# An einsum kernel without its counting instructions, and with 10 KB read twice on eight DMA engines

## Chip, cores and metric

One core of one Trainium2 chip. The metric is device time in microseconds (us) of one execution, the median of several. The profile's *span* runs from the first to the last instruction of the program; the time of an execution is 1.7 to 2.2 us longer than its span, and this difference turns out to matter. Before: 262.18 us, median of 3 runs (261.52 to 262.26).

## The reference

```python
def setup_inputs():
    batch, m, k, n = 16, 512, 768, 1024
    return {"x": randn(batch, k, m), "y": randn(batch, k, n)}      # float32

def reference(x, y):
    return np.einsum('bkm,bkn->bmn', x, y).astype(np.float32)
```

Per batch the core reads 1.5 MB of x and 3 MB of y and writes 2 MB: 109 MB in all.

## The kernel before

VectorE casts x and y to bf16, TensorE multiplies, ScalarE copies PSUM to SBUF, and SyncE issues every transfer. Loads are double buffered; the store of batch b-4 is issued behind the load of batch b. What the change and the argument touch:

```python
    LAG = 4
    NO = 5                                     # output buffers
    ...
    idle = ec(nc.semaphore("idle"))
    ...
    for b in range(B):                         # SyncE
        i = b % 2
        if b >= 2:
            nc.sync.wait_ge(cast, nx[b - 2])
        wide_dma("x", xs[i][:], x_v[b], 4, True).then_inc(sx[i], 16)
        if b >= 2:
            nc.sync.wait_ge(cast, nx[b - 2] + parts(b - 2))
        wide_dma("y", ys[i][:], y_v[b], 2, True).then_inc(sy[i], 16)
        if b >= LAG:
            store(b - LAG)
    for b in range(B - LAG, B - 1):
        store(b)

    for _ in range(60):                        # VectorE counts; nobody waits for it
        nc.vector.sem_inc(idle, 1)
    for b in range(B):
        ...                                    # wait for x, cast; wait for y, cast

    nc.scalar.nop().then_inc(room, 2)
    for _ in range(60):                        # ScalarE counts
        nc.scalar.sem_inc(idle, 1)
    for b in range(B):
        ...                                    # wait for PE, copy PSUM to ob
```

Of the kernel before, what the change touches and what calls it, by code (L numbers as in the profile page):

```python
# [1 line left out]

_os.environ.setdefault("NEURON_RT_ULTRASERVER_MODE", "4")

# [2 lines left out]

# [5 lines left out]


@with_exitstack
def kernel(
    ctx: ExitStack,
    tc: tile.TileContext,
    x: bass.AP,
    y: bass.AP,  # L20
    out: bass.AP,
):
    nc = tc.nc
    P = 128
    FP32 = mybir.dt.float32
    BF16 = mybir.dt.bfloat16

    B, K, M = x.shape
    _, _, N = y.shape
    KT = K // P  # L30
    MT = M // P
    NF = 512
    NT = N // NF



    x_v = x.rearrange("b (p ko) m -> b p ko m", ko=KT)
    y_v = y.rearrange("b (p ko) n -> b p ko n", ko=KT)
    o_v = out.rearrange("b (p mo) n -> b p mo n", mo=MT)

    LAG = 4
    NO = 5
    KH = KT // 2

    section = ExitStack()
    section.enter_context(tc.tile_critical())
    ec = ctx.enter_context
    xs = [ec(nc.sbuf_tensor(f"xs{i}", [P, KT, M], FP32)) for i in range(2)]
    ys = [ec(nc.sbuf_tensor(f"ys{i}", [P, KT, N], FP32)) for i in range(2)]
    xb = ec(nc.sbuf_tensor("xb", [P, 2, KT, M], BF16))  # L50
    yb = ec(nc.sbuf_tensor("yb", [P, 2, KT, N], BF16))
    ob = [ec(nc.sbuf_tensor(f"ob{i}", [P, MT, N], FP32)) for i in range(NO)]

    HB = MT // 2
    ps = [ec(nc.psum_tensor(f"ps{i}", [P, HB, NT, NF], FP32)) for i in range(2)]
    sx = [ec(nc.semaphore(f"sx{i}")) for i in range(2)]
    sy = [ec(nc.semaphore(f"sy{i}")) for i in range(2)]
    so = [ec(nc.semaphore(f"so{i}")) for i in range(NO)]
    cast = ec(nc.semaphore("cast"))
    ready = ec(nc.semaphore("ready"))  # L60
    room = ec(nc.semaphore("room"))
    groups = ec(nc.semaphore("groups"))
    idle = ec(nc.semaphore("idle"))
    outs = ec(nc.semaphore("outs"))


    made = {}

    def wide_dma(key, dst, src, dram_rows, load):


        if key not in made:
            made[key] = nc.sync.dma_start(dst, src)
            return made[key]
        pat = mybir.BassSymbolicTensorAccessPattern
        widen = lambda a: a.rearrange("(q r) k m -> q (r k m)", r=dram_rows)
        plain = lambda a: a.rearrange("p k m -> p (k m)")
        s, d = (widen(src), plain(dst)) if load else (plain(src), widen(dst))
        return nc.sync.add_instruction(_copy.replace(
            made[key].ins, name=nc.get_next_instruction_name(),  # L80
            ins=(pat(ap=s.ap, dtype=s.dtype, bass_ap=s, is_dma=False),),
            outs=(pat(ap=d.ap, dtype=d.dtype, bass_ap=d, is_dma=False),),
            sync_info=None, ant_dge_precooked=False))


    def parts(b):
        return 2 if b in (15,) else 1


    nx = [sum(1 + parts(a) for a in range(b)) + 1 for b in range(B)]  # L90


    def store(b):


        if b < B - 2:
            nc.sync.wait_ge(groups, 2 * (b + 2))
        else:
            nc.sync.wait_ge(outs, b - (B - 3))
        nc.sync.dma_start(o_v[b], ob[b % NO][:]).then_inc(so[b % NO], 16)  # L100

    for b in range(B):
        i = b % 2
        if b >= 2:
            nc.sync.wait_ge(cast, nx[b - 2])
        wide_dma("x", xs[i][:], x_v[b], 4, True).then_inc(sx[i], 16)
        if b >= 2:
            nc.sync.wait_ge(cast, nx[b - 2] + parts(b - 2))
        wide_dma("y", ys[i][:], y_v[b], 2, True).then_inc(sy[i], 16)
# [3 lines that stand above are left out]
        store(b)  # L113


    for _ in range(60):
        nc.vector.sem_inc(idle, 1)
    for b in range(B):
        i = b % 2
        n = 16 * (b // 2 + 1)  # L120
        if b >= 2:
            nc.vector.wait_ge(groups, 2 * (b - 1))
        nc.vector.wait_ge(sx[i], n)
        nc.vector.tensor_copy(xb[:, i], xs[i][:]).then_inc(cast, 1)  # L124
        nc.vector.wait_ge(sy[i], n)
        for h in range(parts(b)):
            ks = slice(h * KT // parts(b), (h + 1) * KT // parts(b))
            nc.vector.tensor_copy(yb[:, i, ks], ys[i][:, ks]).then_inc(cast, 1)  # L128


    for b in range(B):
        nc.gpsimd.wait_ge(cast, nx[b]).then_inc(ready, 1)
        for h in range(parts(b)):
            nc.gpsimd.wait_ge(cast, nx[b] + h + 1).then_inc(ready, 2 // parts(b))


    x_w = xb[:].rearrange("p s k (j mo) -> p s k mo j", mo=MT)
    pe = OrderedEngineSet([nc.tensor.engine])
    with nc.Fori(0, B // 2, engines=pe):
        with nc.Fori(0, 2, engines=pe) as s:  # L140
            nc.tensor.wait_ge(ready, 2).then_inc(ready, -2)
            for mo in range(MT):
                g, m = divmod(mo, HB)
                if m == 0:
                    nc.tensor.wait_ge(room, 1).then_inc(room, -1)  # L145
                for kt in range(KT):
                    if mo == 0 and kt == KH:
                        nc.tensor.wait_ge(ready, 1).then_inc(ready, -1)
                    for nt in range(NT):
                        mm = nc.tensor.matmul(  # L150
                            ps[g][:, m, nt], x_w[:, bass.ds(s, 1), kt, mo],
                            yb[:, bass.ds(s, 1), kt, nt * NF:(nt + 1) * NF],
                            start=(kt == 0), stop=(kt == KT - 1))
                if m == HB - 1:
                    mm.then_inc(groups, 1)


    nc.scalar.nop().then_inc(room, 2)
    for _ in range(60):
        nc.scalar.sem_inc(idle, 1)  # L160
    for b in range(B):
        if b >= NO:
            nc.scalar.wait_ge(so[b % NO], 16 * (b // NO))
        for g in range(2):
            nc.scalar.wait_ge(groups, 2 * b + g + 1)
            cp = nc.scalar.copy(ob[b % NO][:, g * HB:(g + 1) * HB].rearrange("p m (t f) -> p m t f", f=NF),  # L166
                                ps[g][:])
            if b < B - 1:
                cp.then_inc(room, 1)
        if b == B - 2:  # L170
            nc.scalar.drain().then_inc(outs, 1)
    cp.then_inc(outs, 1)

    for b in range(B - LAG - 1, B - 2):
        nc.sync.wait_ge(so[b % NO], 16 * (b // NO + 1))
    section.close()




    nc.sync.dma_start(o_v[B - 1], ob[(B - 1) % NO][:])


# [1 line left out]
_INS = ['x', 'y']  # L185
_OUTS = [((16, 512, 1024), 'float32')]


# [23 lines left out]
```

## Time and profile before

| | before |
|---|---|
| time, median | 262.18 us |
| span of the profiled execution | 260.7 us (an execution of 262.47 us) |
| TensorE busy | 71% |
| DMA queue 1, share of 16 engines | 98.1% |
| instruction packets of queue 14 in the span | 2 |

### The profile page before, as it was taken

What the parts mean: (1) busy time and instruction counts of PE and PEld (TensorE: products, weight loads), DVE (VectorE), ACT (ScalarE), POOL (GpSimd) and SP (SyncE); (2) the same over time, 40 slices, a digit from 0 to 9 for tenths busy, and PEclk for the clock granted to TensorE, in tenths of its full rate; (3) what the DMA queues carried; (4) which work ended last, traced back from release to release, by engine and by line L of the source; (5) the groups of instructions that cost most, each with busy time, mean ns of one, the idle gap of its engine ahead of it and who ended that gap; (6) DMA issues with size and microseconds to landing.
All of it is one profiled execution on the core that took longest, in us unless ns stands there. A gap on an engine that the chain in (4) does not pass through costs nothing. (4 is left out here: it accounts for less than half of the span.)

```text
span 260.7 us, 2506 instructions
## 1 busy us (share of the span) xinstructions
PE 186.1 (71%) x768; PEld 89.8 (34%) x768; DVE 82.0 (31%) x33; ACT 61.1 (23%) x33; POOL 0.2 (0%) x4
## 2 busy tenths in 40 slices
PE   0009999998937949479596894969959197696910
PEld 0004555554512515124242351434425043253500
DVE  0261644525222252312524115252142522225000
ACT  1000442243220222202214022040322205022220
POOL 0000000000000000000000000000000000000000
PEclk9999999999995999959889797797999889799985
DMA  7998999999899899989999989999998999999994
GB/s 260 432 494 385 468 385 468 392 392 488 385 410 493 370 450 475 427 385 405 483 400 437 465 367 453 410 483 402 410 485 382 445 468 417 410 410 430 427 410 181
DMA packets 4514, 109.07 MB, mean 418 GB/s; under 512 B 768, under 2 KB 768, under 8 KB 768
## 3 DMA queue, kind: packets, MB, share of 16 engines
q1 hardware_dynamic: 4512, 109.05, 98.1%
q14 instruction: 2, 0.02, 0.0%
HBM read 75.50 MB, written 33.55 MB: 418 GB/s over the span
## 5 line engine op out<-in xcount | busy, mean ns | idle before, releaser
L150 PE MATMUL ps<-yb,xb 128*128 x768 | 186.1, 407 | 62.7 <-PEq L145 60.7
L150 PEld LDWEIGHTS ps<-yb,xb 128*128 x768 | 89.8, 117 | 158.5 <-issue 92.2
L166 ACT COPY ob<-ps 128x2048 f32<-128x2048 f32 x32 | 59.8, 1870 | 184.2 <-PE ps L150 184.2
L128 DVE CAST yb<-ys 128x6144 bf16<-128x6144 f32 (+1 forms) x17 | 53.8, 3171 | 87.7 <-DMA ys<-in_y_dram 87.7
L124 DVE CAST xb<-xs 128x3072 bf16<-128x3072 f32 x16 | 28.2, 1760 | 69.4 <-DMA xs<-in_x_dram 65.3
L166 ACT ACT_TABLE_LOAD x1 | 1.3, 1283 | 5.3 <-issue 5.3
L196 POOL MEMSET const-bfloat16-1.0<- 128x1 bf16 x1 | 0.1, 102 | 0.0
L196 POOL MEMSET const-uint8-127<- 128x1 uint8 x1 | 0.1, 102 | 0.0
L196 POOL MEMSET const-float32-1.0<- 128x1 f32 x1 | 0.1, 99 | 0.0
L196 POOL MEMSET const-float32-0.0<- 128x1 f32 x1 | 0.1, 98 | 0.2 <-issue 0.2
## 6 DMA issues: line engine op xcount, KB each, us to landing
ys<-in_y_dram SPq DMA_DIRECT2D x16, 3072.0 KB, 28.2
out_dram<-ob SPq DMA_DIRECT2D x16, 2048.0 KB, 32.6
xs<-in_x_dram SPq DMA_DIRECT2D x16, 1536.0 KB, 29.7
```

The lines of the kernel that those rows point to most:

```text
L124: nc.vector.tensor_copy(xb[:, i], xs[i][:]).then_inc(cast, 1)
L128: nc.vector.tensor_copy(yb[:, i, ks], ys[i][:, ks]).then_inc(cast, 1)
L150: mm = nc.tensor.matmul(ps[g][:, m, nt], x_w[:, bass.ds(s, 1), kt, mo], yb[:, bass.ds(s, 1), kt, nt * NF:(nt + 1) * NF], start=(kt == 0), ...
L166: cp = nc.scalar.copy(ob[b % NO][:, g * HB:(g + 1) * HB].rearrange("p m (t f) -> p m t f", f=NF), ps[g][:])
L196: nc = _bacc.Bacc("TRN2", target_bir_lowering=False, num_devices=1)
```

## The change

The intent, as the code shows it: drop 2 x 60 counting instructions that do nothing, and shift eight of the 16 DMA engines against the other eight by a short extra read of 10 KB each, directly behind the first x.

```diff
-    idle = ec(nc.semaphore("idle"))
+    twice = ec(nc.sbuf_tensor("twice", [32, 2560], FP32))
+    sw = ec(nc.semaphore("sw"))
@@ behind the load of x
+        if b == 0:
+            nc.sync.dma_start(twice[::4], y_v[0, 0:32:4].rearrange("p k n -> p (k n)")[:, :2560]).then_inc(sw, 16)
@@ VectorE
-    for _ in range(60):
-        nc.vector.sem_inc(idle, 1)
@@ ScalarE
-    for _ in range(60):
-        nc.scalar.sem_inc(idle, 1)
@@ SyncE, at the end
+    nc.sync.wait_ge(sw, 16)
```

## The prediction

> **What bounds the kernel now.** I read the strip of 40 slices first, because the arithmetic rows of the page say that no compute engine is the limit: TensorE is busy 71% of the span, everything else under 35%.
>
> ```profile
> span 260.7 us, 2506 instructions
> PE 186.1 (71%) x768; PEld 89.8 (34%) x768; DVE 82.0 (31%) x33; ACT 61.1 (23%) x33; POOL 0.2 (0%) x4
> DMA  7998999999899899989999989999998999999994
> DMA packets 4514, 109.07 MB, mean 418 GB/s; under 512 B 768, under 2 KB 768, under 8 KB 768
> q1 hardware_dynamic: 4512, 109.05, 98.1%
> q14 instruction: 2, 0.02, 0.0%
> ```
>
> Queue 1 keeps the 16 DMA engines busy for 98.1% of the span. The second queue matters below: two packets of instructions were fetched inside the span. Next the same by stage (columns: length, busy time and count of PE, PEld, DVE, ACT, POOL, granted clock, DMA share, GB/s):
>
> ```profile
> 0.00:10.00 10.00, 0.00 (x0) 0.00 (x0) 1.76 (x1) 1.28 (x1) 0.20 (x4) 1.00 0.82 320
> 10.00:54.00 44.00, 34.87 (x153) 17.73 (x154) 20.44 (x8) 11.11 (x6) 0.00 (x0) 1.00 1.01 433
> 54.00:235.00 181.00, 139.44 (x564) 66.28 (x563) 56.36 (x23) 43.12 (x24) 0.00 (x0) 0.90 1.00 428
> 235.00:251.00 16.00, 11.78 (x53) 5.77 (x51) 3.43 (x2) 5.60 (x3) 0.00 (x0) 1.00 1.01 431
> 251.00:260.70 9.70, 0.00 (x0) 0.00 (x0) 0.00 (x0) 0.00 (x0) 0.00 (x0) 0.53 0.58 248
> ```
>
> From 10 to 251 us the engines have no gap at all; the only idle DMA time is the first 2 us and the last 9.7 us, where the share falls to 0.58. So each of the 16 engines works off a fixed list without a pause, and the time is that of the engine that finishes its list last. The waits of the issuing queue (columns: waited in total, times, longest) show that the span ends on exactly this:
>
> ```profile
> SPq L207 <- DMA out_dram<-ob: 8.7, 1, 8.7
> ```
>
> The page's own chain of waits stops at the last PSUM copy (250.66 us) and misses this transfer, so I went to the trace's single packet records and to the 16 landing times of each DMA [...]. A 48 KB read takes 1.815 us at best, a 16 KB store packet 0.611, a 12 KB packet of the first x 0.460, a 24 KB packet of the first y 0.912. One engine's list is 8 x 0.460 + 8 x 0.912 + 90 x 1.815 + 128 x 0.611 + 48 x 0.009 = 253.0 us; the first packet starts at 1.98. The records sum to 255.6 us per engine, so 2.6 us per engine are packets that took longer than their best: 1.76 in the 48 KB reads, 0.71 in the first x, 0.19 elsewhere.
>
> The extra is uneven, and that sets the end. The last store's 16 landings are at 256.97 to 257.23 for twelve engines, then 258.01, 258.03, 258.48, and one at 259.90. From the idle time after 255 us the mean end of an engine's packets works out as 257.1; the last packet ends at 259.54. The gap of 2.4 us is paid by everything: span = last packet + 0.36 (landing) + 0.79 (leaving).
>
> Where the straggler starts is visible too. Landing gap between the last engine and the next: none at the first x (0.06), 0.40 at the first y, 0.40 at every load until 52 us, 0.82 at 60, 1.44 at 76, 2.04 at 93, about 2.2 by 125, then 1.4 at the end. Between the first x and the first y lie the two instruction fetches: packets of 8192 B at 9.19 and 11.09 us, 0.309 us each, and the 24 KB packets beginning exactly at their ends took 0.269 and 0.570 us too long. Two engines therefore lose 0.58 and 0.88 us, and the two last landings of the first y, 14.77 and 15.17, are 0.47 and 0.87 after the median. The later steps of the straggler are 48 KB reads that take 0.7 and 0.8 us longer (ends at 59.38 and 75.93 us) while the other engines already store: a late engine becomes later.
>
> [...]
>
> **The change part by part.** *Counting instructions on VectorE:* 60 at 93 ns (0.97 to 6.54 us). VectorE then waits for x anyway until 7.26, so at most 0.7 us before that cast is free: 0 on the path. *On ScalarE:* 60 at 67 ns; they push the table load to 5.34 us, while the first copy runs at 26.38. Also 0 directly:
>
> ```profile
> 5.34 1.28 ACT L166 ACT_TABLE_LOAD   x1 [5.34 <-issue]
> 7.26 1.76 DVE L124 CAST xb<-xs 128x3072 bf16<-128x3072 f32 x1 [7.26 <-DMA xs<-in_x_dram]
> ```
>
> *Their indirect part* is the instruction fetch. ScalarE's counting has one hiccup: the 60th begins 0.38 us after the 59th instead of 0.067, as its 64th instruction in the span, and the fetches follow 4 and 6 us later. [...] Without the padding ScalarE has 114 - 60 = 54 instructions in the span and VectorE 55, so neither gets to its 64th. I expect no fetch inside the span (4 in 5). That takes 0.88 us from the straggler's seed, and part of what it gathered after (2.2 - 0.4).
>
> *The extra read:* 8 rows of 10,240 B[...]. At the rate of the 12 KB packets (0.460 us) that is 10,240 / 12,288 x 0.460 = 0.38 us, plus a 0.009 completion packet: 0.39 us more on each of eight engines, +0.2 on the mean. Issuing it costs SyncE about 0.4 us while the first x is still in flight, so 0. Nothing uses the data, and its wait at the end is long fulfilled. It is pure work on the bound resource, and helps only by shifting two halves of the engines against each other. The first x shows the intended target, I think: eight engines begin by 2.07 us, the rest from 2.07 to 3.05, and the landings form halves with means about 0.27 apart. If the low ones lead, the delay roughly levels them.
>
> *The sum:* mean end 257.1, + 0.2 for the extra read, - 0.1 for the two fetches = 257.2. Distance of the last engine from the mean: 2.4 now. Without the straggler the next are 1.3 and 0.9 over the mean; I take 1.2 with the offset of the low half (0.9 to 1.6). Last packet 258.4, span 258.4 + 1.15 = 259.6, which is 1.1 less than 260.7. The runs' median, 262.18, becomes about 261.0. An earlier end also needs an earlier last issue: the last store is issued at 250.88, 15.2 us after the slowest engine's last y (235.67), and that landing moves with the straggler, so no new bound arises.
>
> **The rivals.** (1) *A new straggler.* The turnarounds from load to store slow reads at random (14 reads lost 0.2 to 0.7 us each at 55 to 59 us, 11 at 119 to 122), and the slowest is slowed further. An offset of 0.39 between halves puts late readers among early writers on purpose. Then the gap stays at 2.4 and the low engines' 0.39 comes on top: 262.2 to 262.6. For it: three other engines drifted 0.8 to 1.3 us behind without any fetch. Against: none of them got to 2. (2) *The offset breaks contention.* At 55 us, when the engines were closest together, the turnaround cost most (about 6.7 of 28 engine-us in all). If the halves no longer collide, the mean falls by up to 1 us more and the time to about 259.5. (3) *The fetch is moved, not removed:* it comes in the middle of the kernel and seeds a straggler later; about 262. (4) *Nothing of this is on the path* because PE or the last copies bound the end: PE's 71% and the unbroken DMA row speak against it; 262.2.
>
> **Range and chances.** Main path 261.0; rivals 1, 3 and 4 end near 262.2 to 262.6, rival 2 near 259.5: a range of 259.5 to 262.5. A 2% gain would mean 256.9, a span of 255.4, under even the mean end of the engines plus leaving: 1 in 100. A 2% loss, 267.4, needs over 5 us of new delay on one engine, twice the present straggler: 1 in 100.
>
> **What would show it.** In the changed kernel: queue 14 has no packet within the span; queue 1 has 16 more packets and 0.08 MB more; the table load moves to about 1 us; the gap of the last engine at the first y falls under 0.3 us; the spread of the last store's landings falls from 2.9 to under 2. The prediction is wrong if fetches remain, if one engine is again over 2 us behind, or if the mean end of the engines moves by more than 0.7 us from 257.2.

Marked gaps in the recorded texts, here and below, are cuts of what no trace or run of this case shows. The forecast's sum: a mean end of 257.1 + 0.2 - 0.1 = 257.2, a last engine 1.2 later, span 259.6, median about 261.0. Three things in it are the author's reading. That each of a transfer's 16 landings is one engine's: the profile before has 768 landings for its 48 transfers, and 768 packets of 4 B at 0.009 us, the "completion packets" of the sum. That the eight engines of the extra read are the "low" ones: no trace names an engine, so "low", here and in twice_x4, means no more than the eight that take it. And that the two fetches have to do with ScalarE's 64th instruction of the span, which began 0.38 us after the one before it, so that none comes where neither ScalarE nor VectorE has so many: an estimate from that one profile.

## More of the kernel before

The DMA share says that all 16 DMA engines work nearly all the time, so a row of the busy times of the compute engines says little about the end. The lines are in the prediction. The one line that belongs beside them is who TensorE's input waits for (columns: waited in total, times, longest), from the waits of VectorE in the kernel before:

```profile
DVE yb L128 <- DMA ys<-in_y_dram: 87.7, 16, 6.2
DVE xb L124 <- DMA xs<-in_x_dram: 65.3, 13, 7.3
```

VectorE waited for data at each of the 16 y loads: compute follows the transfers. The changed kernel's lines are nearly the same:

```profile
DVE yb L131 <- DMA ys<-in_y_dram: 87.1, 16, 6.1
DVE xb L127 <- DMA xs<-in_x_dram: 65.6, 13, 7.3
```

## The result, and the profile after

262.57 us median of 6 runs (261.50 to 262.80), against 261.94 (261.06 to 262.26) for the kernel before in 6 runs: a ratio of 1.0024, 95% interval 1.0001 to 1.0046. Ratios here are the mean time of one kernel's fast runs over the mean of the other's fast runs of the same rounds, so they are not quite the ratio of the medians. The change is a small loss of some 0.6 us; forecast was a gain of 1.2.

The page of the changed kernel, the lines that answer to those of before:

```profile
span 260.3 us, 2388 instructions
PE 191.3 (73%) x768; PEld 90.7 (35%) x768; DVE 82.0 (31%) x33; ACT 61.1 (23%) x33; POOL 0.2 (0%) x4
DMA  6999989899999899899999989999998998989994
DMA packets 4528, 109.14 MB, mean 419 GB/s; under 512 B 776, under 2 KB 776, under 8 KB 776
q1 hardware_dynamic: 4528, 109.14, 98.2%
```

There is no line of queue 14 any more: no instruction fetch in the span. Queue 1 has the 16 forecast packets more. The same by stage (length, busy time and count by engine, granted clock, DMA share, GB/s):

```profile
0.00:10.00 10.00, 0.00 (x0) 0.00 (x0) 1.76 (x1) 1.28 (x1) 0.20 (x4) 1.00 0.81 323
10.00:54.00 44.00, 35.41 (x156) 18.04 (x157) 20.48 (x8) 11.25 (x6) 0.00 (x0) 1.00 1.00 429
54.00:235.00 181.00, 144.50 (x564) 67.12 (x563) 56.32 (x22) 42.97 (x23) 0.00 (x0) 0.86 1.00 429
235.00:251.00 16.00, 11.35 (x51) 5.53 (x49) 3.43 (x2) 5.60 (x3) 0.00 (x0) 1.00 1.00 427
251.00:260.30 9.30, 0.00 (x0) 0.00 (x0) 0.00 (x0) 0.00 (x0) 0.00 (x0) 0.50 0.63 268
```

Still no idle DMA time from 10 to 251 us. The start, in order of time (start, duration, engine, line, operation, idle time before and what ended it):

```profile
0.95 0.38 SPq L74 DMA_DIRECT2D xs<-in_x_dram  x1
0.97 1.28 ACT L167 ACT_TABLE_LOAD   x1 [0.97 <-SPq L46]
1.39 0.80 SPq L111 DMA_DIRECT2D twice<-in_y_dram  x1
2.23 0.40 SPq L74 DMA_DIRECT2D ys<-in_y_dram  x1
7.34 1.76 DVE L127 CAST xb<-xs 128x3072 bf16<-128x3072 f32 x1 [7.34 <-DMA xs<-in_x_dram]
```

The table load now comes at once, 4.4 us earlier, and the first cast starts no earlier (7.34 against 7.26): counting delayed nothing. Issuing the extra read took 0.80 us, not 0.4, against 0.38 to 0.62 for the loads around it, still inside the first x; why, is not shown. Its semaphore has nine recorded updates: one at 2.56 us, when none of its packets had started (the first does at 6.13), and eight from 6.90 to 7.23. The end hangs on the same wait as before (waits of the issuing queue):

```profile
SPq L209 <- DMA out_dram<-ob: 8.7, 1, 8.7
```

Two things in these traces answer the prediction. First, the engines. From the packet records and the landing times (each transfer lands 16 times, in the author's reading once per engine), the spread between the first and the last engine, of the load or store that lands about then:

| us from the start | before | after | loads only (below) | stores in pairs (below) |
|---|---|---|---|---|
| 14 (first y) | 1.22 | 0.42 | 0.58 | 1.23 |
| 51 (last load before stores) | 1.23 | 0.41 | 0.58 | 1.22 |
| 83 | 2.26 | 0.63 | 0.58 | 1.86 |
| 115 | 2.86 | 0.93 | 0.58 | 1.87 |
| 146 | 3.33 | 1.49 | 0.58 | 1.88 |
| 178 | 3.49 | 1.98 | 0.58 | 1.93 |
| 209 | 3.51 | 2.68 | - | 2.09 |
| last store | 2.93 | 2.72 | - | 2.71 |

The changed kernel starts with a third of the spread and ends with nearly the same. The small start is not the work of the missing fetches alone: no_count (below), also without fetches but without the extra read, has 0.88 us there. The last engine is made on the way: in the packet records, from 120 us on, there is one read of 48 KB per batch or so that takes 0.34 to 0.64 us too long (at 120.6, 136.6, 152.8, 168.0, 184.1, 185.0 and 216.1 us), while other engines already store; not each of these falls on the engine that ends last. (Queue 1 does not name its engines. What can be read is how late the last landing of each transfer is.)

Second, the time outside the span. Each timed execution has both numbers. After: 2.13 to 2.22 us, mean 2.19, in 6 runs. For the kernel before these pairs came only with the experiments: 1.75 to 1.82, mean 1.78, in 11. So part of the loss is in no line of the page. Whether it lies before the first instruction or after the last, these two numbers do not say.

### The profile page after: what moved, and what is told of

Same layout as the page of the kernel before. It is cut to its first block, busy times and chain, and to the rows that moved or that the text cites. A ratio compares the mean times of both kernels' runs of the same rounds, so it can differ in the third digit from the quotient of the medians.

```text
span 260.3 us, 2388 instructions
## 1 busy us (share of the span) xinstructions
PE 191.3 (73%) x768; PEld 90.7 (35%) x768; DVE 82.0 (31%) x33; ACT 61.1 (23%) x33; POOL 0.2 (0%) x4
## 5 line engine op out<-in xcount | busy, mean ns | idle before, releaser
L153 PE MATMUL ps<-yb,xb 128*128 x768 | 191.3, 415 | 57.1 <-PEq L148 55.1
```

The source lines that it names most:

```text
L153: mm = nc.tensor.matmul(ps[g][:, m, nt], x_w[:, bass.ds(s, 1), kt, mo], yb[:, bass.ds(s, 1), kt, nt * NF:(nt + 1) * NF], start=(kt == 0), ...
```

## The experiments

Theory A: the last engine regrows from any start, and the removal gains nothing. Theory B: the counting had a use, outside the span. The twelve runs came in four calls, each on one chip with its own runs of the kernel before; "span" and "outside" (time minus span) are means over a kernel's fast runs, from the numbers listed with each run. The spans of one kernel differ by up to 1.7 us from execution to execution (count_act: 259.8 to 261.5), so a difference of two mean spans is uncertain by some 0.3 to 0.7 us, an estimate from their scatter; paired scatters less. The outside times of one kernel lie within 0.2 us.

| run | time, median | before, median | ratio (95%) | span | outside |
|---|---|---|---|---|---|
| before, first (11 runs) | 262.32 | | | 260.55 | 1.78 |
| after_again | 263.03 | 262.32 | 1.0021 (1.0009 to 1.0034) | 260.82 | 2.18 |
| no_count | 262.73 | 262.32 | 1.0016 (1.0001 to 1.0032) | 260.55 | 2.17 |
| twice_count | 262.67 | 262.32 | 1.0014 (1.0002 to 1.0026) | 260.85 | 1.82 |
| count_act | 262.67 | 262.32 | 1.0014 (0.9995 to 1.0033) | 260.62 | 2.16 |
| before, second (11 runs) | 262.31 | | | 260.55 | 1.78 |
| count_dve | 262.15 | 262.31 | 1.0001 (0.9988 to 1.0013) | 260.28 | 1.95 |
| dve_5 | 262.08 | 262.31 | 1.0004 (0.9989 to 1.0019) | 260.23 | 2.11 |
| dve_20 | 262.52 | 262.31 | 1.0005 (0.9992 to 1.0017) | 260.52 | 1.96 |
| dve_end | 262.30 | 262.31 | 0.9987 (0.9970 to 1.0004) | 260.10 | 1.98 |
| before, third (9 runs) | 261.98 | | | 260.19 | 1.78 |
| loads_only (wrong) | 204.50 | 261.98 | 0.7806 (0.7791 to 0.7820) | 202.35 | 2.15 |
| paired | 261.50 | 261.98 | 0.9981 (0.9968 to 0.9995) | 259.74 | 1.79 |
| twice_x4 | 262.91 | 261.98 | 1.0031 (1.0017 to 1.0045) | 261.04 | 1.79 |
| before, fourth (11 runs) | 261.57 | | | 259.87 | 1.76 |
| paired_20 | 261.75 | 261.57 | 1.0003 (0.9983 to 1.0023) | 259.93 | 1.76 |

**after_again**: the changed kernel, unchanged.

> The changed kernel once more, to place its time and its last engine. Theory A (straggler regrows whatever the start, the time outside the span is equal): ratio to before within 0.998 to 1.003 and, as often as not, no difference; time minus span the same in both kernels. Theory B (part of the time has moved to outside the span, since the instruction fetch that the padding had caused inside it now falls elsewhere): ratio 1.001 to 1.004, time minus span about 2.2 us here and about 1.8 in the kernel before, spans about equal or 0.4 us shorter here.

The loss came again, 1.0021. Theory B's numbers held for the ratio and for the outside time (2.18); its span did not, since it rose by 0.27. The profile of this repeat is the plainest answer to the prediction: no fetch in the span, a spread under 0.6 us from the first y until 51 us, and at the end one engine that lands 2.21 us behind the next (260.58 after 258.36). In the kernel before, with its fetches, that gap was 1.41.

**no_count**: the removal alone.

```diff
-    idle = ec(nc.semaphore("idle"))
...
-    for _ in range(60):
-        nc.vector.sem_inc(idle, 1)
...
-    for _ in range(60):
-        nc.scalar.sem_inc(idle, 1)
```

> Counting instructions removed, no extra read. Theory A: no fetch packets inside the span, landing spread of the second load under 0.8 us, the straggler regrows to over 2 us at the end, time within 0.5 us of before. Theory B: the time minus span is 2.2 us as in the changed kernel, and the time is 0.2 to 0.6 us over before. My theory on record (fetch seeds the straggler and it stays away without it): 1.0 to 1.5 us under before.

The mean span is that of before, 260.55, and the outside time is 2.17. That they agree to the hundredth is luck: by the scatter of the runs the difference of the spans lies within some 0.5 us of zero (dve_5 below, also without a fetch in the span, is 0.31 under its before, and as uncertain). A gain of 1.0 to 1.5 us is excluded. No 8 KB instruction packet falls in the span; the one packet of queue 14 on this page has 32 B and comes at 0.03 us, and other kernels have it just before their span:

```profile
DMA packets 4513, 109.06 MB, mean 419 GB/s; under 512 B 769, under 2 KB 769, under 8 KB 769
q14 instruction: 1, 0.00, 0.0%
```

The profiled execution starts with a spread of 0.88 us and still ends with 2.91. Its lateness is shared: the last engine lands only 0.21 us behind the next, but 2.0 behind the mean. So in the span the removal is worth nothing that these runs show, and the 0.39 us that it costs is outside. My theory falls here.

**twice_count**: the extra read alone, with the counting kept.

```diff
+        if b == 0:
+            nc.sync.dma_start(twice[::4], y_v[0, 0:32:4].rearrange("p k n -> p (k n)")[:, :2560]).then_inc(sw, 16)
...
+    nc.sync.wait_ge(sw, 16)
```

> Extra read added, counting instructions kept. Theory A: two fetch packets remain, the time is before plus 0 to 0.4 us (the extra read is on eight engines). Theory B: time minus span is 1.8 us as before. If the offset of halves breaks contention: 0.5 to 1 us under before.

The span rises by 0.30 us and the outside time stays (1.82). The profile of this run also tests whether the last copy bounds the end:

```profile
DMA  6999999999999899999999989999998999999985
```

In it the last product took 12.23 us instead of 10.72 (the granted clock was 0.59 from 238 to 242 us), so the last store was issued at 252.37 instead of 250.88, and the DMA share fell to 0.55 from 250 to 253 us, against 0.96. Yet the last landing came at 259.94, against 259.90 in the kernel before: the last engine was busy with its own list until then (the store before had landed at 255.10 there, 255.09 in the kernel before). Fourteen of the 16 landings, though, had moved to 258.5 to 258.7, where twelve had been by 257.2, so the last store's issue is a second limit not far behind. (This is one profile against one.)

The two parts of the change add up: 0.27 to 0.30 for the read and 0.39 for the counting make 0.66 to 0.69; after_again is 0.66 above before in the mean (262.99 against 262.33).

**count_act**: counting on ScalarE only.

```diff
-    for _ in range(60):
-        nc.vector.sem_inc(idle, 1)
```

> Counting on ScalarE alone. [...] if each engine causes one of the two fetch packets, one remains here and one engine of the first y lands late; if ScalarE causes both, both remain. Time within 0.5 us of before under A; under B the time minus span lies at 1.8 if ScalarE's fetch is the one that counts, at 2.2 if VectorE's is, at 2.0 if each brings half.

One fetch remains, at 9.05 us, and count_dve (next) has one too, at 10.02: each engine's padding causes one packet. From the page of this run:

```profile
q1 hardware_dynamic: 4512, 109.05, 98.1%
q14 instruction: 1, 0.01, 0.0%
```

The outside time is 2.16: ScalarE's padding alone helps nothing.

**count_dve**: counting on VectorE only.

```diff
-    for _ in range(60):
-        nc.scalar.sem_inc(idle, 1)
```

> All 60 counting instructions on VectorE, none on ScalarE. From the last four runs: time minus span was 1.78 and 1.82 us with VectorE's padding and 2.16 to 2.18 without. Theory B (VectorE's padding alone saves about 0.39 us outside the span): time minus span 1.78, one fetch packet in the span, span as in the kernel before within 0.3, time equal to before within 0.3 us. Rival (both engines' padding is needed): time minus span 2.17, time 0.4 us over before.

Neither number expected: 1.95, between the two. Together with the runs before: none 2.17, ScalarE alone 2.16, VectorE alone 1.95, both 1.78. This is how a maximum behaves, not a sum: if each unpadded engine comes late, VectorE by 0.39 and ScalarE by 0.17, helping only the earlier of the two shows nothing. That the lateness is of this kind is argued from the four numbers, not seen.

**dve_5**: only five on VectorE, none on ScalarE.

```diff
-    for _ in range(60):
+    for _ in range(5):
         nc.vector.sem_inc(idle, 1)
@@ ScalarE
-    for _ in range(60):
-        nc.scalar.sem_inc(idle, 1)
```

> Five counting instructions on VectorE: 60 instructions of VectorE in the span. Theory B1 [...]: no fetch packet in the span, time minus span 2.17. Rival B2 (any counting at the start, or its delay, brings the gain): time minus span 1.8 or in proportion, 2.14.

B1, as these runs test it, is that a fetch comes behind a fixed place among VectorE's instructions, at about the 64th of the span (ScalarE's 64th in the kernel before began 0.38 us after its 63rd, the others 0.067 us apart); this place is called the boundary from here on.

Outside 2.11; no queue-14 line on the page. But the packet records, which go on past the span, have one packet of 8192 B at 261.67 us, 1.8 us after this execution's span ended (259.9). The fetch was not avoided: here it fell into the few microseconds in which the program leaves, 1.84 us after VectorE's 60th and last instruction of the span (259.83). The recorded semaphore updates of that stretch end at 2.02 us after the span instead of 1.90 in the kernel before.

**dve_20**: the same with twenty.

> Twenty counting instructions on VectorE: 75 instructions in the span, over the supposed boundary. B1: one fetch packet, at a time when VectorE has done its 64th instruction (batch 13 or so, near 200 us, since 20 are counted at the start), time minus span 1.78. B2: time minus span about 2.04, in proportion to the count.

The fetch came at 201.03 us. VectorE's 61st instruction of the span stands at 196.81, just ahead of the cast that this line of its timeline shows:

```profile
196.87 1.76 DVE L124 CAST xb<-xs 128x3072 bf16<-128x3072 f32 x1 [5.24 <-DMA xs<-in_x_dram]
```

Outside 1.96, as with sixty on VectorE. In every trace with such packets inside the span each follows VectorE's 61st or ScalarE's 62nd instruction of the span by 3.8 to 5.3 us, so the boundary lies about there (in dve_5 the packet came sooner, behind the 60th). It is a position in the program, not the counting at the start, that matters; B2's 2.04 did not come, and dve_end (next), which counts nothing at the start, settles it.

**dve_end**: sixty on VectorE, behind its last cast.

```diff
-    for _ in range(60):
-        nc.vector.sem_inc(idle, 1)
     for b in range(B):
         ...
+    for _ in range(60):
+        nc.vector.sem_inc(idle, 1)
```

> Sixty counting instructions on VectorE behind its last cast. B1: one fetch packet after VectorE's last cast (about 240 us), and time minus span 1.78, as the boundary is still crossed before the program ends; if the fetch comes too late to help, between 1.78 and 2.17. B2 (it is the start that matters): 2.17. For the span: with no fetch at the start it should be as in the run without counting, 260.5.

Fetch at 240.68, outside 1.98. The expected 1.78 was wrong for the same reason as in count_dve: ScalarE is not covered. Its mean span, 260.10, is lower than before's, but the interval of the ratio includes 1, so nothing follows from that.

**loads_only**: no counting, no extra read, and no store but the last. Its output is wrong, which doesn't matter for the time. The question is whether reads alone make a late engine.

```diff
-        nc.sync.dma_start(o_v[b], ob[b % NO][:]).then_inc(so[b % NO], 16)
+        pass
...                                            # and the waits for these stores, and the counting
```

> No counting, no extra read, and no stores but the last (wrong result on purpose). Theory S (an engine falls behind where its reads meet the other engines' stores): the spread of the landings stays as the first loads leave it, under 1.2 us, to the last load, and 48 KB reads over 2.0 us are absent. Rival R (reads slow one engine in any case): the spread grows to over 2 us here too. Span about 109.05 - 31.5 MB at the loads' rate: 187 to 192 us.

The spread stays at 0.58 us from the first x to the last load, and none of the 1440 reads of 48 KB takes over 0.1 us too long. The stage table, DMA share 1.00 as before:

```profile
10.00:54.00 44.00, 35.58 (x156) 18.01 (x157) 20.48 (x8) 11.27 (x6) 0.00 (x0) 1.00 1.01 435
54.00:175.00 121.00, 116.27 (x531) 59.95 (x530) 56.32 (x22) 41.17 (x22) 0.00 (x0) 1.00 1.00 429
```

Its partner with stores is no_count, where the spread grew from 0.88 to 3.24 us. Theory S holds: the late engine is made where there are stores between the reads. This run also corrects the sum in the prediction: its reads still took 25 us over their best in total, evenly (about 0.017 each), so not all of the "1.76 us per engine" was delay. In the kernel before, 49 reads that took over 0.1 us too long make up 16.8 of the 28.1 us; the rest, 0.7 us per engine, is spread over all reads. The span was longer than expected, 202.4, because the last store could be issued only after the last product.

**paired**: the kernel before with stores issued two at a time.

```diff
-    NO = 5
+    NO = 6
-        if b >= LAG:
+        if b > LAG and b % 2:
+            store(b - LAG - 1)
             store(b - LAG)
```

> The kernel before with stores issued two at a time behind every second load (six output buffers instead of five): half as many changes between loads and stores in the middle. Theory S: fewer meetings of reads and stores, so less extra time in 48 KB reads (under 20 us in sum against 25 to 35) and a last engine 1 to 1.5 us behind instead of 2 to 3; span 259.3 to 260.0 against 260.55. Rival (the number of changes does not matter, or the longer burst makes the late engine later): 260.5 or more.

Faster than before: 0.9981 (0.9968 to 0.9995), span 259.74 against 260.19. The page:

```profile
span 259.8 us, 2505 instructions
DMA  7998999999999999999999999999999999999994
DMA packets 4514, 109.07 MB, mean 420 GB/s; under 512 B 768, under 2 KB 768, under 8 KB 768
q1 hardware_dynamic: 4512, 109.05, 98.3%
q14 instruction: 2, 0.02, 0.0%
```

The DMA row has not one slice under 9 from the fifth to the last but one, but no_count has only one and is no faster, so the gain isn't read from this row. All 16 engines lose 0.2 to 1.1 us at the first meeting of reads and stores (66 to 70 us, 11.9 us in all); after that only two reads lose over 0.1 us, at 163.6 and 195.3. But two forecasts did not come. The 48 KB reads lost 30.5 us in all, not under 20, against 28.1 in the kernel before: less is lost in long reads (12.4 against 16.8) and more in small amounts. And the last engine is not "1 to 1.5 us behind": in the stores at the end the spread grows from 2.1 to 2.7, and the last landing is 1.8 us after the mean, against 2.4 in the kernel before. The sixth buffer and the later stores came with the pairing and were not tried alone.

**twice_x4**: counting kept, and four such reads.

```diff
+            for j in range(4):
+                nc.sync.dma_start(twice[j::4], y_v[0, j:32:4].rearrange("p k n -> p (k n)")[:, :2560]).then_inc(sw, 16)
```

> Counting kept as before, and four such extra reads instead of one: 4 x 0.39 = 1.57 us on each of the eight low engines. Theory W (the extra read is plain work on the bound engines, about 0.28 us of span per read as the one read showed): span 1.1 to 1.6 us over before, time minus span 1.8. Rival O (the offset of the halves matters as such, not the work): no rise in proportion; 0 to 0.4 over, or under.

The span rises by 0.85 us (261.04 against 260.19): 0.21 per read, against 0.30 for one. More packets on the page:

```profile
q1 hardware_dynamic: 4576, 109.38, 98.1%
```

Four reads are 1.57 us more on eight engines, and the span pays about half. Something comes back: the reads of 48 KB that took over 0.1 us too long lost 5.8 us in all in this trace, 12.0 to 16.9 in the three profiles with one extra read (after, after_again, twice_count), and 16.8 to 24.8 in the seven without it that store one at a time. That is no proof, but it points one way: the offset reduces such delays, by less than it costs.

**paired_20**: paired stores and twenty counting instructions on both engines, to put their 61st instruction near 200 us instead of at the start.

```diff
-    for _ in range(60):
+    for _ in range(20):
         nc.vector.sem_inc(idle, 1)
...
-    for _ in range(60):
+    for _ in range(20):
         nc.scalar.sem_inc(idle, 1)
```

> Stores in pairs, and 20 counting instructions on each of VectorE and ScalarE instead of 60[...]. [...] two fetch packets near 200 us, none at the start, time minus span 1.78 as with 60 (both engines covered). For the span: if the fetches at the start cost nothing lasting, as the earlier runs say, it stays at 259.5 to 260.0 and the time at 261.3 to 261.8; if they do seed the last engine in this version, 259.2 or less. Faster than both kernels of the case either way.

The outside time is 1.76, equal to before's: with both engines over the boundary, where they cross it makes no difference to the time outside. The fetches came at 195.43 and 234.85 us, behind VectorE's 61st instruction (190.18) and ScalarE's 62nd (230.74). But the version isn't faster: 1.0003. Its span (259.93) and its time (261.75) lie in the forecast ranges, but on this chip the kernel before is at 259.87 and 261.57: "faster than both" failed. In its profile the packets that follow the two fetches lost 0.47 and 0.21 us. The last engine's distance to the next was 0.73 us before the first of them, 0.51 after it, then 1.01 two stores later and 1.74 at the end; a like step, from 0.34 to 0.67, came at two stores before any fetch. So whether the late fetches cost time here, and whether they or the different chip took away the gain of paired, is open.

## Why the prediction was wrong

- **No fetch in the span, 16 more packets, no delay from the counting itself**: right. The table load moved to 0.97 us, the first cast did not move.
- **Where the last engine starts**: right in part. Without the fetches, and with the extra read, the first y landed within 0.42 us instead of 1.22 (0.88 in no_count, where the fetches alone are gone), and the last engine there was 0.04 us behind the next instead of 0.40. Two readings were off: the two last landings of the first y come 0.39 and 0.79 us after the median of 14.38, not 0.47 and 0.87; and the two packets were not both for ScalarE: each engine's counting brings one (9.05 us in count_act, 10.02 in count_dve).
- **Distance of the last engine, "I take 1.2"**: this is the step that failed. By the prediction's own measure, last packet minus mean end, it is 2.1 us in the profile after (259.17 and 257.04), 2.5 in after_again and 2.0 in no_count, against 2.4 before (259.54 and 257.11). The prediction took the lag for a legacy of the fetches; it grows without them. loads_only shows where: with no stores between the reads the spread stays at 0.58 us. In after_again one engine of a pack that began within 0.6 us ended 2.21 us behind the next, which meets the prediction's own sign of being wrong; of its signs of being right, the spread of the last store "under 2" failed (2.72 in the profile after). The prediction had this as rival 1 and gave it too little, arguing that the engines without a fetch had drifted only "0.8 to 1.3 us".
- **Mean end 257.2**: right, 257.04 in the profile. **Extra read as pure work**: right in kind; its packets took 0.385 us each, as worked out, and the span rose by 0.27 and 0.30 us for one read and 0.85 for four (the last is clear of the scatter).
- **"Span = last packet + 0.36 + 0.79"**: right, 1.13 after. **That the median moves as the span does**: wrong, and the missing term. Taking the counting out adds 0.39 us outside the span. That VectorE and ScalarE both have to be over the boundary for the small outside time is shown (2.17, 2.16, 1.95, 1.78). Why is not. The likely reading is that the counting had moved the two fetches into the program and that without it they fall into the leaving, but only dve_5 has such a packet in its records; in the changed kernel the semaphore updates recorded past the span end 1.90 us after it, as in the kernel before, and nothing there is later.
- **The sum**: forecast, relative to before, +0.2 for the read, -0.1 for the fetches, -1.2 for the last engine, 0 outside. The runs: +0.3, then 0 for the fetches and the last engine together (within some 0.5 us), and +0.39. The base was a little high, too: the profile of before was an execution of 262.47 us, slower than all six of its timed runs of the first result.
- **The rivals**: 1 came in its outcome, a last engine as late as ever. That its 262.2 to 262.6 holds the 262.57 measured is partly luck: 0.39 us of it is the time outside, which no rival had, and the offset made long reads no more frequent, as rival 1 has it. 2 is seen in small (twice_x4). 3 did not come: the changed kernel has no fetch in its span. 4 does not fit twice_count, where the last store was issued 1.5 us later and the end stayed.

## What to carry to other kernels

Where every transfer engine was busy to the end, the span ended with the slowest engine (in the kernel before twelve of the last store's landings had come by 257.23 us, the last came at 259.90, and the span was 260.7): look at the spread of the landings of one transfer over time, and find the stage in which it grows before you remove what seems to have started it. Fewer changes between loads and stores (paired) gained 0.45 us of span, where a better alignment at the start gained nothing; paired_20, on another chip, did not repeat the gain. And take time minus span for each run: instructions that do nothing decided here where a fetch fell (9.19 and 11.09 us with sixty on both engines, 201.03 with twenty on VectorE, 1.8 us after the span with five), and the page doesn't show what lies outside the span.
